# Two scan directions in one ordered list, and a block inverse that sums only the columns a step still changes, in place in one tile

## The chip, the cores and the metric

The kernel runs on one core of one Trainium2 chip. The metric is the device time of one launch in microseconds, lower is better; three runs of the kernel before lie between 3606.57 and 3625.46 us, with a median of 3611.12. Engines are named as the profile does: PE (TensorE), DVE (VectorE), ACT (ScalarE), POOL (GpSimd), SP (SyncE, whose queue issues nearly all DMAs).

## The reference

One layer of a hybrid backbone for 4096 latent and 256 context tokens of width 1024. A modulated, normalised stream is projected once; half of the result feeds a bidirectional RWKV-7 mixer (8 heads of 64, one scan a direction), the other half a gMLP on chunks of 128 tokens; both are gated, concatenated, projected back and added to the input. Cut to what matters here:

```python
def _delta_scan(r, k, v, decay, kk, kka, s0, reverse):
    def step(s, inp):
        r_t, k_t, v_t, w_t, kk_t, b_t = inp
        sa = jnp.einsum('bhvk,bhk->bhv', s, -kk_t)
        s = (s * w_t[:, :, None, :] + sa[..., None] * b_t[:, :, None, :]
             + v_t[..., None] * k_t[:, :, None, :])
        return s, jnp.einsum('bhvk,bhk->bhv', s, r_t)
...
    for d in range(2):
        ...
        y_d, s_d = _delta_scan(r, k_d, v, decay, kk, kk * a, s0[d], reverse=(d == 1))
        y = y + y_d
        bonus = bonus + jnp.sum(r * k_d * p['r_k'][d].astype(f32), axis=-1, keepdims=True) * v
        finals.append(s_d)
...
    y = (y - mu) * lax.rsqrt(var + GN_EPS) * hv(p['gn_w']) + hv(p['gn_b']) + bonus
...
    mixed = jnp.concatenate([y_a * jax.nn.silu(z_a), y_b * jax.nn.silu(z_b)], axis=-1)
    out = mixed @ p['w_out']
    return x + _rmsnorm(out, p['ln_post']) * gate, s_f, s_b
```

The context runs after the latent tokens in this kernel's lists, from a zero state; its final states are outputs.

## The kernel before

**Stages.** Modulation, normalisation, input projection and token shift come first and write their results to DRAM (0 to some 1340 us). Then phase2 runs the forward scan over 34 tiles of 128 tokens and, beside it, the projection for the gMLP (two tiles at a time, `proj`, lines 1031 to 1066). Then phase3 runs the backward scan over the 34 tiles (latent tiles from the last to the first, then the context) with group norm, gating and the output projection (`part`, line 1260). Below, F0 to F33 are the forward tiles and B0 to B33 the backward ones, in the order in which they run.

**One tile.** The recurrence over 64 tokens is solved in closed form, as a triangular system for each head. `prep_ops` makes the gates, the decays, the operands Z and X, and by PE (`ab`, line 769) and a masked product on DVE (`abm`, line 777) the matrices AB, all heads in one 128-partition tile. `invert_ops` then inverts 64x64 unit-triangular blocks. `diag` (line 786) sends the 16x16 diagonal blocks to DRAM by eight DMAs, and `blocks` (line 821) brings them back as rows in Ab. Fifteen steps on DVE (`step0` to `step14`, a product at line 851 and a subtraction at 855 each) invert all the diagonal blocks at once in TP. `keepT` (line 859) and `place` (line 864, eight DMAs) carry the result through DRAM into Qb, `flip` (line 880) transposes it, and four groups of matmuls `mm0` to `mm3` (line 873, each 16 products of 64x64 operands), with `wm` (line 884, masks the first) and `ym0` to `ym2` (line 893, Qb minus the product) between them, sum the series for the blocks off the diagonal. Every one of these works on all 64 columns of a head; ym0 and ym1 write tiles Y, ym2 writes Tt. `scan_ops` applies it to the state S, one 64-token chunk after the other (`zs`, `av`, `xsc`, `tu`, `uv`, `sm`, `ys`, `su`, `so`). `bon` (line 794) is the bonus: q as the weights, two columns of rkb moving; `bonc` (line 798) copies the eight sums a token. In the forward scan ACT copies the output into yt (line 1091) and `keep` (line 1094) stores it to DRAM.

**What sets the order.** `pipeline` collects the parts of all tiles of one direction with a due time, PERIOD (30 units) times the tile's number plus an entry of a table (AT_FWD, AT_PROJ, AT_BWD), sorts them, and emits them under a schedule that keeps this order on each engine and each queue:

```python
            evs += [(self.PERIOD * n + at[k], f) for k, f in parts.items()]
        with self.tc.manual_schedule():
            for _, f in sorted(evs, key=lambda e: e[0]):
                f()
```

So a tile's preparation, inverse and application overlap those of its neighbours within a direction, and a waiting instruction holds all that follows on its engine. DMAs of SP's queue use eight semaphores in turn (DMAHW0 to DMAHW7 in the rows of order below), and one waits for the landing of the one eight before it.

**Between the directions.** phase2 and phase3 have a `scan_setup` and pools of their own. phase3 starts with the broadcast of the gate vector (`load_gp`, lines 1121 to 1125: eight diagonal tiles `dg` on DVE, eight products on PE), loads gn_w and gn_b on ACT's queue (lines 1131, 1136), and loads w_out in eight pieces through one slot `wst`, each split into a rounded part and a rest for two-pass products (`split_w`: DMA line 243, ACT cast line 244, DVE subtraction line 245). Only then comes the second list. `load_state` (lines 583 to 587) fetches and transposes the initial state when the first tile needs it.

## Time and profile before

| | us |
|---|---|
| median of three runs | 3611.12 (3606.57 to 3625.46) |
| the profiled execution | 3635.12 |
| its span | 3633.4 |
| PE busy | 3238.2 (89%) |
| PE weight loads busy | 2692.5 (74%) |
| DVE busy | 2059.3 (57%) |
| ACT busy | 1219.5 (34%) |
| POOL busy | 1005.1 (28%) |

The profile is one execution as the hardware profiler saw it. Engines work beside each other, so busy times don't add up to the span, and matmul ends are modelled. The granted clock of TensorE is 1.00 at full speed. Rows of a timeline give start and duration, and in brackets the idle time of the engine just before and what ended it.

### The profile page before, as it was taken

How to read it: one execution, taken by the hardware profiler on the slowest of the kernel's cores; microseconds unless marked ns; L12 is line 12 of the kernel's file. 1: busy time of each engine (PE TensorE's matmuls, PEld its weight loads, DVE VectorE, ACT ScalarE, POOL GpSimd, SP SyncE). 2: the span in 40 equal slices, each digit the busy share in tenths (PEclk: the TensorE clock that was granted, in tenths of full speed). 3: DMA queues.
4: the chain of work that ended last, by engine and by line, in shares of the span. 5: the costliest groups of instructions: out<-in, count | busy, mean ns of one | idle time of the engine just before them, and what ended most of it. 6: DMA issues, size and time to landing. Idle time of an engine off the chain costs nothing. (4 is left out here: it accounts for less than half of the span.)

```text
span 3633.4 us, 102021 instructions
## 1 busy us (share of the span) xinstructions
PE 3238.2 (89%) x43093; PEld 2692.5 (74%) x43093; DVE 2059.3 (57%) x4969; ACT 1219.5 (34%) x2928; POOL 1005.1 (28%) x1500
## 2 busy tenths in 40 slices
...
GB/s 261 139 194 154 144 184 168 160 99 93 128 87 99 64 117 95 110 103 118 91 119 99 111 109 104 110 55 104 85 108 120 116 116 119 117 112 113 119 116 69
DMA packets 526870, 429.61 MB, mean 118 GB/s; under 512 B 191051, under 2 KB 458187, under 8 KB 519244
## 3 DMA queue, kind: packets, MB, share of 16 engines
...
q14 instruction: 119, 0.97, 0.1%
HBM read 275.46 MB, written 147.46 MB: 116 GB/s over the span
## 5 line engine op out<-in xcount | busy, mean ns | idle before, releaser
L1042 PE MATMUL acc<-hld,wAh 128*128 128x256 f32 x2176 | 434.7, 300 | 13.3 <-DMA hld<-d_h 13.3
L1042 PEld LDWEIGHTS acc<-hld,wAh 128*128 128x128 f32 x2176 | 356.6, 201 | 25.1 <-DMA hld<-d_h 16.2
L1042 PE MATMUL acc<-hld,wAl 128*128 128x256 f32 x1088 | 317.6, 292 | 0.0
L851 DVE TENSOR_TENSOR tm<-TP,Ab 128x48 f32<-128x48 f32 (+13 forms) x1020 | 218.1, 214 | 156.1 <-DMA Ab<-dA 126.6
L777 DVE TENSOR_TENSOR AB<-prep,mask 128x512 f32<-128x512 f32 x272 | 177.1, 683 | 125.1 <-PE prep L769 122.0
L855 DVE TENSOR_TENSOR TP<-TP,tm 128x48 f32<-128x48 f32 (+13 forms) x1020 | 225.4, 221 | 35.1
L1260 PE MATMUL acc<-wAh,mh 128*128 128x512 f32 x544 | 242.1, 445 | 3.0 <-DVE on L1286 2.9
L272 PE MATMUL acc<-hl,wAh 128*128 128x512 f32 (+1 forms) x576 | 226.0, 395 | 0.0
L724 POOL TENSOR_TENSOR q<-q,k 128x512 f32<-128x512 f32 x68 | 97.3, 1431 | 457.5 <-ACT q L719 348.2
L1260 PE MATMUL acc<-wAl,mh 128*128 128x512 f32 x544 | 220.2, 405 | 0.0
L1260 PE MATMUL acc<-wAh,ml 128*128 128x512 f32 x544 | 220.1, 405 | 0.0
L272 PE MATMUL acc<-hh,wAl 128*128 128x512 f32 (+1 forms) x576 | 218.6, 384 | 0.0
L1042 PEld LDWEIGHTS acc<-hld,wAl 128*128 128x128 f32 x1088 | 217.8, 200 | 0.0
L272 PE MATMUL acc<-hh,wAh 128*128 128x512 f32 (+1 forms) x576 | 217.7, 393 | 0.0
L769 PE MATMUL prep<-Z,X 64*64 64x128 f32 x4352 | 169.2, 283 | 47.6 <-DVE X L755 42.0
L272 PE MATMUL acc<-hld,wAh 128*128 128x512 f32 (+1 forms) x576 | 175.9, 389 | 16.5 <-ACT wAh L244 11.7
L758 POOL TENSOR_TENSOR q<-q,r 128x512 f32<-128x512 f32 x68 | 99.0, 1455 | 327.5 <-DVE X L755 241.7
L465 PE MATMUL acc<-wAh,hld 128*128 128x512 f32 x544 | 183.6, 402 | 0.0
L769 PEld LDWEIGHTS prep<-Z,X 64*64 64x64 f32 x4352 | 129.7, 137 | 72.5 <-issue 34.8
L253 ACT COPY win<-acc 128x512 f32<-128x512 f32 (+1 forms) x108 | 60.7, 564 | 351.6 <-PE acc L272 334.7
L873 PE MATMUL inv<-Y,W 64*64 64x64 f32 x4352 | 160.8, 224 | 18.4 <-DVE Y L893 17.9
L465 PE MATMUL acc<-wzh,hld 128*128 128x512 f32 x544 | 176.0, 394 | 0.0
...
## 6 DMA issues: line engine op xcount, KB each, us to landing
...
```

Of the source, the lines that this page charges most:

```text
L253: nc.scalar.copy(w[:, 2 : 2 + n], ps[:, :n])
L272: self.nc.tensor.matmul(ps[:, :n], a[:, k, :], b[:, k, :n], start=(k == 0 and j == 0), stop=(k == NK - 1 and j == 2),)
L465: nc.tensor.matmul(ps, a[:, k, sub], b[:, k % 2, :], start=(k == 0 and j == 0), stop=(k == NK - 1 and j == 2),)
L724: nc.gpsimd.tensor_mul(fl(P["q"]), fl(P["q"]), fl(P["k"]))
L758: nc.gpsimd.tensor_mul(fl(P["q"]), fl(P["q"]), fl(P["r"]))
L769: nc.tensor.matmul(P["pab", pi][hh][o, 128 * p : 128 * p + 128], w, self.slots(P["Z"], p, pi, hh), start=True, stop=True, tile_position=(6 ...
L777: nc.vector.tensor_mul(P["AB"][:, x, 4 * pi : 4 * pi + 4, :], P["pab", pi][hh].rearrange("p (a b) -> p a b", a=4), m)
L851: nc.vector.tensor_mul(tm[:, :nj, :nt], TP[:, js, s : s + 1].to_broadcast([128, nj, nt]), Ab[:, s : s + 1, tt].to_broadcast([128, nj, nt]),)
L855: nc.vector.tensor_sub(TP[:, js, tt], TP[:, js, tt], tm[:, :nj, :nt])
L873: nc.tensor.matmul(ps[h, 64 * j : 64 * j + 64], l(x, h, j), r[h, j, :], start=True, stop=True, tile_position=(64 * x, 64 * x),)
L1042: nc.tensor.matmul(Q["ps", j][:, b, :], x[:, k, :], y[:, k, :], start=(k == 0 and i == 0), stop=(k == NK - 1 and i == 2),)
L1260: nc.tensor.matmul(P["po"][half], a[:, ki, :], b[:, ki % 2, :], start=(ki == 4 and j == 0), stop=(ki == 3 and j == 2),)
```

## The change

**One list.** `scan_setup` runs once. `direction(d)` makes what differs between the directions (moff, the constants ka2 and rkb, a zeroed tile W), for both ahead of the list, on POOL. `forward` and `backward` return their parts, `scans` sorts them together. The first backward tile stands at `turn()`, 1030.14 units, that is 34 periods and 10.14, so that its preparation stands among the steps of the last forward tiles. `origin(1)` and `triangle(1)` set run0, inc and the mask for the second direction in place, on POOL, inside the list. The pieces of w_out are loaded by SP and split by ACT and POOL from 975.6 units on, into two slots in turn, which like gp, gn, zs, x and the rest of the backward buffers are slices of tiles that the projection's inputs leave free. The gn loads move to SP. The states are fetched ahead and the forward state is stored just before B0's first product.

**Columns.** Of four groups of matmuls, mm0 and mm1 now produce 48 of 64 columns, mm2 32 and mm3 16; wm and the ym work on the same columns. wm writes into the direction's W, whose other columns stay zero, and the ym write in place into Tt, whose first 16 columns (the last 16 backward) ACT copies from Qb (`yown`). The tiles Y are gone.

**Bonus.** rkb becomes the weights (32 columns, two of them filled) and q moves with 128 columns, four products into four quarters of the partitions; ACT copies the result out (`bonr`), PE transposes it (`bont`), and `bonc` reads the eight columns.

**Table.** In the forward table `keep`, the store of yt, moves from 70.37 to 42.50.

```diff
+    def turn(self):
+
+        T = self.PERIOD
+        after = (("su1", "zs0"), ("ys1", "zs0"), ("so0", "zs0"), ("so1", "zs1"), ("cum", "gates00"), ("up", "up"))
+        after += tuple((f"abm{i}", "ab0") for i in ("00", "01", "10", "11"))
+        return T * (self.NT // 128) + 3.0 + max(0.0, *(self.AT_FWD[a] + 0.1 - T - self.AT_BWD[b] for a, b in after))
...
+    def direction(self, d):
+
+        nc, io, st = self.nc, self.io, self.sst
+        c = SimpleNamespace(d=d)
...
+        c.W = st.tile([128, 8, 64], F32, name=f"W{d}")
+        nc.gpsimd.memset(c.W, 0.0)
+        c.ka2 = st.tile([128, 4], F32, name=f"kb{d}")
+        c.ka = self.vT[:, 64 + 4 * d : 68 + 4 * d]
+        nc.gpsimd.tensor_scalar(c.ka2, c.ka, -1.0, 2.0, op0=ALU.mult, op1=ALU.add)
+        c.rkb = st.tile([128, 4, 32], F32, name=f"rkb{d}")
+        nc.gpsimd.memset(c.rkb, 0.0)
+        rk = self.vT[:, 72 + 4 * d : 76 + 4 * d]
+        for hh in range(2):
+            sl = slice(64 * hh, 64 * hh + 64)
+            nc.gpsimd.tensor_scalar_mul(c.rkb[sl, :, hh], rk[sl], 0.25)
...
-    def load_state(self, src):
+    def fetch_state(self, t, src):
+        t = self.stio = t[0:64].rearrange("v (p x) -> v p x", p=4)
+        self.nc.sync.dma_start(t.rearrange("v p (h k) -> v p h k", h=2), src.rearrange("(p h) v k -> v p h k", h=2))
+
+    def load_state(self, zero):
         nc = self.nc
-        if src is None:
+        if zero:
             nc.gpsimd.memset(self.S, 0.0)
             return
-        t = self.s1.tile([64, 4, 128], F32, name="stin", tag="q")
-        nc.sync.dma_start(t.rearrange("v p (h k) -> v p h k", h=2), src.rearrange("(p h) v k -> v p h k", h=2))
         ps = self.px.tile([128, 256], F32, name="us", tag="us")
         for p in range(4):
-            nc.tensor.transpose(ps[:, 64 * p : 64 * p + 64], t[:, p, :], self.ident[:64, :64])
...
-        "ys1": 23.38, "sm1": 23.82, "su1": 25.37, "so1": 42.35, "keep": 70.37,
...
+        "keep": 42.50,
...
         def bon():
-            P["pb"] = pb = psum()
-            pbv = pb[:, 0:8].rearrange("t (h p) -> t p h", h=2)
+
+            P["pb"] = psum()
             for p in range(4):
-                nc.tensor.matmul(pbv[:, p, :], P["q"][:, p, :], self.rkb[:, p, :], start=True, stop=True)
+                nc.tensor.matmul(
+                    P["pb"][32 * p : 32 * p + 32, 0:128], c.rkb[:, p, :], P["q"][:, p, :], start=True, stop=True,
+                    tile_position=(0, 32 * p),
+                )
+
+        def bonr():
+            P["br"] = s1.tile([128, 128], F32, name="br", tag="br")
+            nc.scalar.copy(P["br"], P["pb"][:, 0:128])
+
+        def bont():
+            P["pt8"] = psum()
+            nc.tensor.transpose(P["pt8"][:, 0:128], P["br"], self.ident)
 
         def bonc():
             P["bo"] = s2.tile([128, 8], F32, name="bo", tag="bo", bufs=3)
-            nc.vector.tensor_copy(P["bo"], P["pb"][:, 0:8])
+            nc.vector.tensor_copy(
+                P["bo"].rearrange("t (h p) -> t p h", h=2),
+                P["pt8"][:, 0:128].rearrange("t (p x) -> t p x", p=4)[:, :, 0:2],
+            )
 
...
+        cols = lambda a: slice(16 * a, 64) if d == 0 else slice(0, 64 - 16 * a)
+        low = slice(0, 48) if d == 0 else slice(16, 64)
+        own = slice(0, 16) if d == 0 else slice(48, 64)
+        j8 = lambda t: t.rearrange("p (j t) -> p j t", j=8)
+
+        def mm(i, l, r, cc):
             ps = P["pi", i] = self.px.tile([128, 512], F32, name="inv", tag="inv")
             for j in range(8):
                 for x in range(2):
                     h = slice(64 * x, 64 * x + 64)
                     nc.tensor.matmul(
-                        ps[h, 64 * j : 64 * j + 64], l(x, h, j), r[h, j, :],
+                        j8(ps)[h, j, cc], l(x, h, j), r()[h, j, cc],
                         start=True, stop=True, tile_position=(64 * x, 64 * x),
                     )
...
         def wm():
-            P["W"] = s1.tile([128, 8, 64], F32, name="W", tag="W")
             nc.vector.tensor_mul(
-                P["W"], P["pi", 0].rearrange("p (j t) -> p j t", j=8),
-                fl(self.moff).unsqueeze(1).to_broadcast([128, 8, 64]),
+                P["c"].W[:, :, low], j8(P["pi", 0])[:, :, low],
+                fl(P["c"].moff)[:, low].unsqueeze(1).to_broadcast([128, 8, 48]),
             )
-            P["Y"] = self.Qb
+
+        def yown():
+            P["Tt"] = self.s2.tile([128, 8, 64], F32, name="Tt", tag="Tt")
+            nc.scalar.copy(P["Tt"][:, :, own], self.Qb[:, :, own])
 
         def ym(i):
-            tag = "Tt" if i == 2 else "Y"
-            Y = P["Y"] = self.s2.tile([128, 8, 64], F32, name=tag, tag=tag)
-            nc.vector.tensor_sub(fl(Y), fl(self.Qb), P["pi", i + 1])
-            if i == 2:
-                P["Tt"] = Y
+            cc = cols(i + 1)
+            nc.vector.tensor_sub(P["Tt"][:, :, cc], self.Qb[:, :, cc], j8(P["pi", i + 1])[:, :, cc])
 
         order = list(range(15) if d == 0 else range(15, 0, -1))
...
-    def pipeline(self, order, pp, more, at, extra=()):
-
-        evs = list(extra)
+    def pipeline(self, n0, order, c, pp, more, at):
+
+        evs = []
         for n, t0 in enumerate(order):
-            P = dict(t0=t0)
+            P = dict(t0=t0, c=c)
             begin, sink, own = more(n, P)
             parts = {
                 **self.load_ops(P), **self.prep_ops(P, pp), **self.invert_ops(P), **self.scan_ops(P, begin, sink), **own,
             }
-            evs += [(self.PERIOD * n + at[k], f) for k, f in parts.items()]
-        with self.tc.manual_schedule():
-            for _, f in sorted(evs, key=lambda e: e[0]):
...
+    def scans(self):
+
         with ExitStack() as ctx:
             hp = self.pool(ctx, "h2", bufs=3)
             op = self.pool(ctx, "o2", bufs=2)
             pp = self.pool(ctx, "p2", bufs=2, space=PSUM)
-            self.scan_setup(ctx, 0)
-
-            ws = []
+            self.scan_setup(ctx)
+            self.load_up(0)
+            self.origin(0)
+            self.triangle(0)
+            evs = self.forward(hp, op, pp, self.direction(0))
+            evs += self.backward(hp, op, pp, self.direction(1))
+            T, N = self.PERIOD, self.NT // 128
+            evs += [
+                (T * (N - 1) + self.AT_FWD["up"] + 0.01, lambda: self.load_up(1)),
+                (self.turn() + self.AT_BWD["gates00"] - 0.01, lambda: self.origin(1)),
+                (self.turn() + self.AT_BWD["ab0"] - 0.01, lambda: self.triangle(1)),
+            ]
+            with self.tc.manual_schedule():
+                for _, f in sorted(evs, key=lambda e: e[0]):
+                    f()
+
...
+        def load_gp(b):
+            dgs = self.s2.tile([128, 2, 128], F32, name="dg", tag="xs")
+            for half in range(2):
+                pg = pp.tile([128, 512], F32, name="prep", tag="prep")
+                for k4 in range(4):
+                    k = 4 * half + k4
+                    dg = dgs[:, k4 % 2]
+                    nc.vector.tensor_scalar_mul(dg, self.ident, self.gl[:, k, b : b + 1])
+                    nc.tensor.matmul(pg[:, 128 * k4 : 128 * k4 + 128], self.ones, dg, start=True, stop=True)
...
+        def load_w(i):
+            q, half = units[i]
+            src = io["w_out"][0, :, 512 * half : 512 * half + 512]
+            st = box[2 * (i % 2)][:, 0:1024].rearrange("p (k n) -> p k n", k=2)
+            if q < 2:
+
+                v = src[0:512].rearrange("(k a h c) n -> h a c k n", k=2, a=2, h=2)[q]
+                for a in range(2):
+                    nc.sync.dma_start(st[64 * a : 64 * a + 64], v[a])
+            else:
+                nc.sync.dma_start(st, src[256 * q : 256 * q + 256].rearrange("(k p) c -> p k c", p=128))
+
+        def split(i):
+            st = box[2 * (i % 2)][:, 0:1024].rearrange("p (k n) -> p k n", k=2)
+            hi, lo = (self.wA.tile([128, 2, 512], F32R, name=f"wo{x}", tag="wA") for x in "hl")
+            ws[units[i]] = (hi, lo)
+            nc.scalar.copy(hi, st)
+            nc.gpsimd.tensor_sub(lo, st, hi.bitcast(F32))
...
+        at = T * (N - 2) + max(self.AT_PROJ.values()) + 0.1
+        evs += [(at, room), (at + 0.01, lambda: load_gn(0)), (at + 0.02, lambda: load_gn(1)), (at + 10.0, half_gn)]
+        evs += [(at + 0.03 + 6 * i, lambda i=i: load_w(i)) for i in range(8)]
+        evs += [(at + 7.5 + 6 * i, lambda i=i: split(i)) for i in range(8)]
+        evs += [
+            (at + 54.0, lambda: load_gp(0)),
+            (self.turn() + self.AT_BWD["zs0"] - 12.0, lambda: self.fetch_state(box[2][:, 1536:2048], io["state_bwd"][0, 0])),
+            (self.turn() + self.AT_BWD["zs0"] - 0.02, lambda: self.store_state(box[2][:, 1024:1536], io["new_state_fwd"][0, 0])),
+            (self.turn() + T * N + 3 * T, lambda: self.store_state(box[2][:, 1024:1536], io["new_state_bwd"][0, 0])),
...
+                P["bv"] = box[3]
...
+                P["zs"] = box[2][:, 1024:1536]
...
+        order = list(range(self.TS - 128, -1, -128)) + list(range(self.NT - 128, self.TS - 1, -128))
+        evs += self.pipeline(self.turn() / T, order, c, pp, more, self.AT_BWD)
+        return evs
```

On SP, in the forward scan at an odd tile, the store of the output (d_yf) and keepT (dT<-TP) stand like this before:

```order
L657 DMA lw<-d_lora 128x128 [waits PE_49]
L1094 DMA d_yf<-yt 128x512 [waits DMAHW6_49,Activation_49]
L1049 DMA s<-d_s 128x256 [waits DMAHW7_49,DMAHW1_49]
L859 DMA dT<-TP 2x64x128 [waits DMAHW0_49,DVE_49]
L1049 DMA s<-d_s 128x256 [waits DMAHW2_49]
```

and like this after; the store has moved behind a load of the gMLP gate (s) to just ahead of keepT.

```order
L687 DMA lw<-d_lora 128x128 [waits PE_49]
L1121 DMA s<-d_s 128x256 [waits DMAHW7_49,DMAHW2_49,Pool_49]
L1164 DMA d_yf<-yt 128x512 [waits DMAHW0_49,Activation_49]
L904 DMA dT<-TP 2x64x128 [waits DMAHW1_49,DVE_49]
L1121 DMA s<-d_s 128x256 [waits DMAHW3_49]
```

On POOL, at the start of the backward direction, before: the masks come first, then the products q of B0.

```order
L519 AFFINE_SELECT mask<-ones 64x64 [waits DMAHW2_49,PE_49]
L519 AFFINE_SELECT mask<-ones 64x64 [waits Pool_49]
L519 AFFINE_SELECT mask<-ones 64x64 x6
L527 AFFINE_SELECT moff<-ones 64x64 x2
L553 AFFINE_SELECT eye<-ones 64x128 x2
L559 MEMSET Qb 128x512 [waits Pool_49]
L1060 TENSOR_TENSOR s<-s,th 128x256 [waits DMAHW6_49,DMAHW3_49,DVE_49]
L736 COPY gc<-G 128x8
L580 MEMSET S 128x256
L736 COPY gc<-G 128x8 [waits DMAHW3_49,DMAHW4_49,DMAHW2_49,DMAHW5_49,DMAHW1_49,DMAHW6_49,DMAHW0_49,DMAHW7_49,Activation_49,Pool_49]
L724 TENSOR_TENSOR q<-q,k 128x512 [waits DMAHW4_49,Activation_49]
L758 TENSOR_TENSOR q<-q,r 128x512 [waits DMAHW5_49,DVE_49]
```

After, the first subtraction of w_out (wol) stands between B0's two q products, and the selects of the mask behind them:

```order
L755 TENSOR_TENSOR q<-q,k 128x512 [waits DMAHW5_49,Activation_49,Pool_49]
L1236 TENSOR_TENSOR wol<-box_26262,woh 128x1024 [waits DMAHW1_49,DMAHW0_49,Activation_49]
L789 TENSOR_TENSOR q<-q,r 128x512 [waits DMAHW6_49,DVE_49]
L889 COPY TP<-eye 128x128
L558 AFFINE_SELECT mask<-ones 64x64
L558 AFFINE_SELECT mask<-ones 64x64 [waits Pool_49]
L558 AFFINE_SELECT mask<-ones 64x64 x6
```

On SP at the same place, before, the last pieces of w_out and B0's diag (dA<-AB), where each load waits for DVE's subtraction:

```order
L243 DMA wst<-in_w_out 128x2x512 [waits DMAHW5_49,DMAHW4_49,DVE_49]
L243 DMA wst<-in_w_out 128x2x512 [waits DMAHW6_49,DVE_49]
L243 DMA wst<-in_w_out 128x2x512 [waits DMAHW7_49,DMAHW0_49,DVE_49]
L786 DMA dA<-AB 16x8x16 [waits DMAHW1_49,DVE_49]
L786 DMA dA<-AB 16x8x16 x3
L786 DMA dA<-AB 16x8x16 [waits DVE_49]
L786 DMA dA<-AB 16x8x16 x2
```

and after, the second and third piece ahead of B0's diag, where the third waits for POOL; the others have moved ahead of F33's place or behind diag.

```order
L1227 DMA box_26264<-in_w_out 64x2x512 [waits DMAHW4_49]
L1227 DMA box_26264<-in_w_out 64x2x512 [waits DMAHW5_49]
L1227 DMA box_26262<-in_w_out 64x2x512 [waits DMAHW6_49,Pool_49]
L1227 DMA box_26262<-in_w_out 64x2x512 [waits DMAHW7_49]
L1167 DMA d_bf<-bo 128x8 [waits DMAHW0_49]
L817 DMA dA<-AB 16x8x16 [waits DMAHW1_49,DVE_49]
L817 DMA dA<-AB 16x8x16 [waits DMAHW2_49]
```

On PE, in the forward scan, the bonus between the products of the state and the second ab, before:

```order
L970 MATMUL us<-UV,tk 64x64 [waits PE_49]
L970 MATMUL us<-UV,tk 64x64 x7
L794 MATMUL prep<-rkb,q 128x2 [waits DVE_49,Pool_49]
L794 MATMUL prep<-rkb,q 128x2 x3
L769 MATMUL prep<-Z,X 64x128 [waits DVE_49] x2
L769 MATMUL prep<-Z,X 64x128 x14
```

and after, with the transpose behind it; ab's products have moved behind an instruction that waits for ACT.

```order
L1025 MATMUL us<-UV,tk 64x64 [waits PE_49]
L1025 MATMUL us<-UV,tk 64x64 x7
L825 MATMUL prep<-q,rkb_9193 32x128 [waits DVE_49,Pool_49]
L825 MATMUL prep<-q,rkb_9193 32x128 x3
L836 MATMUL prep<-ident,br 128x128 [waits DVE_49,Activation_49]
L800 MATMUL prep<-Z,X 64x128 [waits PE_49]
L800 MATMUL prep<-Z,X 64x128 [waits DVE_49]
L800 MATMUL prep<-Z,X 64x128 x14
```

## Rows read from the trace of the kernel before

**Rows 1.** Head of the page: span and instructions of the profiled execution.
```profile
span 3633.4 us, 102021 instructions
```

**Rows 2.** Windows: from:to length, then busy (instructions) by engine, clock, DMA, GB/s.
```profile
core 0: us, PE busy (x) PEld busy (x) DVE busy (x) ACT busy (x) POOL busy (x), PEclk, DMA share, GB/s
1450.00:2360.00 910.00, 822.29 (x16473) 768.05 (x16471) 581.22 (x1570) 346.73 (x926) 126.78 (x174) 0.97 0.39 107
...
2450.00:2640.00 190.00, 118.46 (x1940) 97.71 (x1942) 107.57 (x276) 67.56 (x165) 44.06 (x68) 0.69 0.36 92
...
2640.00:3530.00 890.00, 815.85 (x14955) 661.96 (x14951) 717.72 (x1948) 430.79 (x1144) 405.19 (x621) 0.98 0.42 116
```

**Rows 3.** Timeline of DVE: first instruction of step0 for F0, F1, F33, B0, B1, B2.
```profile
1379.48 0.18 DVE L851 TENSOR_TENSOR tm<-TP,Ab 128x15 f32<-128x15 f32 x1 [3.86 <-DMA Ab<-dA]
...
1414.51 0.15 DVE L851 TENSOR_TENSOR tm<-TP,Ab 128x15 f32<-128x15 f32 x1
...
2416.12 0.17 DVE L851 TENSOR_TENSOR tm<-TP,Ab 128x15 f32<-128x15 f32 x1 [2.54 <-DMA Ab<-dA]
...
2511.16 0.17 DVE L851 TENSOR_TENSOR tm<-TP,Ab 128x15 f32<-128x15 f32 x1 [7.89 <-DMA Ab<-dA]
...
2547.58 0.17 DVE L851 TENSOR_TENSOR tm<-TP,Ab 128x15 f32<-128x15 f32 x1
...
2579.71 0.17 DVE L851 TENSOR_TENSOR tm<-TP,Ab 128x15 f32<-128x15 f32 x1
```

**Rows 4.** Chain of waits between the scans: start, duration, what held the end.
```profile
2468.51 1.05 ACT wAh L244
...
2471.49 4.08 DMA wst<-in_w_out
...
2497.29 3.66 DMA wst<-in_w_out
...
2503.91 7.16 DMA Ab<-dA
```

**Rows 5.** Instructions by line on POOL: busy us, mean ns, then idle before.
```profile
L218 POOL TENSOR_TENSOR hl<-ht,hh 128x512 fp32r<-128x512 f32 (+1 forms) x72 | 94.0, 1320 | 96.4 <-ACT hh L217 96.4
L519 POOL TENSOR_SCALAR_AFFINE_SELECT mask<-ones 64x64 f32<-64x64 f32 x16 | 3.8, 235 | 4.3 <-PE acc L465 3.6
```

**Rows 6.** Timeline of DVE: the forward state's copy, and a diagonal of load_gp.
```profile
1412.10 0.42 DVE L587 COPY S<-us 128x256 f32<-128x256 f32 x1 [7.46 <-PE us L586]
...
2464.93 0.29 DVE L1121 TENSOR_SCALAR dg<-ident,gl 128x128 f32<-128x128 f32 x1 [1.16 <-PE prep L1122]
```

**Rows 7.** Timeline of SP and DVE: the DMA part of backward tile B16's loop.
```profile
3012.15 0.54 SPq L821 DMA_DIRECT2D Ab<-dA  x1
...
3016.47 0.68 DVE L893 TENSOR_TENSOR Tt<-Qb,inv 128x512 f32<-128x512 f32 x1
...
3018.00 0.17 DVE L851 TENSOR_TENSOR tm<-TP,Ab 128x15 f32<-128x15 f32 x1 [0.85 <-DMA Ab<-dA]
```

**Rows 8.** Timeline of PE in the forward scan: bursts of the inverse, of ab, of bon.
```profile
2219.50 1.15 PE L873 MATMUL inv<-Qb,W 64*64 64x64 f32 x32
...
2243.28 1.10 PE L769 MATMUL prep<-Z,X 64*64 64x128 f32 x32
...
2245.28 1.02 PE L794 MATMUL prep<-rkb,q 128*128 128x2 f32 x8 [0.27 <-DVE AB L777]
```

**Rows 9.** Timeline of ACT and SP: an even forward tile (two rows), then an odd one.
```profile
2200.19 0.74 ACT L1091 COPY yt<-xy 64x256 f32<-64x256 f32 x2
...
2206.76 0.54 SPq L859 DMA_DIRECT2D dT<-TP  x1
...
2238.17 0.54 SPq L859 DMA_DIRECT2D dT<-TP  x1
...
2240.33 0.75 ACT L1091 COPY yt<-xy 64x256 f32<-64x256 f32 x2
...
2242.07 3.75 SPq L864 DMA_DIRECT2D Qb<-dT  x8
...
2248.43 5.50 SPq L786 DMA_DIRECT2D dA<-AB  x8
```

576 lines of the change are left out of this document (280 added, 296 removed), and 49 rows, old and new, of tables (AT_BWD, AT_FWD).

## The prediction

> **What bounds the kernel now.** I read the page first: a span of 3633.4 us [rows 1]. The windows by stage come next [rows 2]. They tempt one to call the kernel TensorE-bound: PE is busy 822 of 910 us in the forward scan and 816 of 890 in the backward scan, DVE only 581 and 718. The third window, between the scans, is different: PE is busy 118 of 190 us and its clock falls to 0.69. I call it the seam.
>
> The DVE timeline shows the beat of both scans [rows 3]. The first instruction of the block inverse (step0, line 851) of forward tile F1 starts at 1414.51 and that of the last, F33, at 2416.12: 32 periods of 31.3 us. The backward tiles go as fast: B2 at 2579.71, B16 at 3018.00 [rows 3, 7], 14 periods of 31.3. From F33 to B0, however, there are 95.0 us, and from B0 to B1 36.4.
>
> What sets the 31.3 is a loop that rows 7 and 9 let one follow: step0 and the 14 steps after it on DVE, further DVE work up to the last masked product (abm, line 777) of the next tile, eight DMAs to DRAM (diag, line 786), one DMA back (blocks, line 821), and step0 of the next tile, which waits for that landing. In rows 7 blocks is issued at 3012.15 and step0 starts at 3018.00, after DVE has idled 0.85 us for Ab; the last subtraction of the inverse (ym2, line 893) ended before that. So PE's 90% is cover, not bound, and what DVE does between diag and step0 is cover as well, as long as step0 still waits for Ab.
>
> The seam is a chain of its own [rows 4]. The output weights go through one staging slot: load, cast on ACT (1.05), subtraction on DVE, then the next load. From the load at 2471.49 to the one at 2497.29 there are four such turns of 6.45 us, some 4 of them a landing. B0's blocks stand on SP behind the loads, at 2503.91, and land 7.2 us later.
>
> **The seam.** After the change there is one ordered list, so that B0's preparation runs under F33's steps and the loads begin at once behind F33's store of its diagonal blocks. An undisturbed turn would be one period, 31.3 us. On top of it I put what now stands in B0's way. On POOL, between B0's q product and its mask, there is the first subtraction, 128x1024, twice the 1.32 us of 128x512 at line 218, and then eight selects of 0.235 that turn the mask round [rows 5]: 2.64 + 1.88 = 4.5, and abm of B0 on DVE waits for the last of them. On SP four gn loads and eight halves of w_out stand between F33's keepT and B0's blocks: 12 issues at 0.54, as line 821 took one [rows 7], are 6.5, of which about 1 lies where place waits for keepT's landing anyway. 31.3 + 4.5 + 5.5 = 41.3; I take 41, so 95.0 - 41 = **-54**. Bounds: if POOL's piece is hidden, 31.3 + 5.5 = 36.8, say 36 (-59). If one load that waits for its slot to be free (landing 4.08, cast 1.05, subtraction 2.64, together 7.8) is waited out in front of diag, where the third load indeed waits for POOL, 49, say 50 (-45).
>
> From B0 to B1 the other four loads move into B0's and B1's turns. I put that distance at 32.5, near B1 to B2's 32.1 [rows 3]: **-3.9** (-4 to +6, the price of one waited load, which rival C uses). The broadcast of the gate vector (load_gp) leaves the gap and enters DVE's part of B1's loop: eight diagonals of 0.29 [rows 6]. Without waits that is 2.3 us; with the 1.16 that DVE idled before one for PE [rows 6], 8 x 1.45 = 11.6. I take **+3.5**, nearer the low end, since there are two slots now and a product can run under the next diagonal.
>
> **The start.** The state load of the forward scan was issued in the middle of F0, and DVE sat 7.46 us behind its transposes [rows 6]; F0 to F1 took 35.0 instead of 31.3 [rows 3]. It is now fetched 30 units before the tile, so I give back 3.5: **-3.5** (0 to -5). The constants of both directions are now built by POOL ahead of the list, some six more small ones at about 0.24 [rows 5]: **+1** (0 to 3).
>
> **The column cut.** On DVE the four instructions behind the matmuls (lines 884 and 893) go from 512 columns to 384, 384, 256 and 128. A 128x512 takes 0.68 [rows 7] and a PSUM read of 128x256 0.42 [rows 6], about 1.0 ns a column, so 0.13 + 0.13 + 0.26 + 0.40 = 0.9 us a tile. In the backward scan all of it stands between diag and step0, where step0 waits for Ab anyway: worth the few tiles in which it does not. I take **-2** for the direction (-6 to +6: a new wait could come with the copy of the own columns, which now stands on ACT ahead of the products). On PE 256 columns a pair of operands become 144, but that costs the same: 32 matmuls of line 873 on 64 columns take 1.15 us and 32 of line 769 on 128 columns 1.10, and eight of line 794 on 2 columns 1.02 [rows 8]. I count zero.
>
> **The forward scan.** Here one wait goes and one comes. ym2 stands among the next tile's steps, so its 0.4 us is on the loop: -0.4 in every tile. But the store of yf (line 1094) is moved from after the next tile's turn to right before keepT (line 859) on SP, and it waits for ACT's copy into yt (line 1091). SP is in order: behind it wait keepT, the loads of UV, the eight place DMAs (line 864) and diag. In even tiles the copy ended at 2200.93 and keepT came at 2206.76 [rows 9]: nothing. In odd tiles, where the copy stands behind the gMLP gate, keepT was issued at 2238.17 and the copy ended at 2241.08 [rows 9]: 2.9 us of waiting, with the store's own issue 3.4. Place ended at 2245.82, one further issue behind it ends at 2246.4, and diag began at 2248.43 [rows 9], so 2.0 of it is slack: +1.4, less ym2's 0.4; this tile's copy is a late one, and I take +0.8. 17 x (-0.4) + 17 x 0.8 = **+7** (-14, if slack swallows it all, to +16, if half a microsecond of it is missing).
>
> **The bonus.** Four weight loads of q with 2 columns become four of the small weights with 128, an ACT copy and a transpose. PE gets through the eight old instructions in 1.02 [rows 8]; the new detour lies behind the masked products, and in the forward scan diag waits for place longer than for AB, in the backward scan bonc stands behind diag. I count zero.
>
> The Trainium skill speaks against that: "TensorEngine Tiling (Array Packing)", section Key Properties, says that a change of the tiling mode, not only of the tile, drains the engine. The trace shows at most 0.27 us of idle PE before line 794, and that is put down to DVE [rows 8]; it neither proves nor excludes a drain. By the rule the sum would get rival D's addition.
>
> **Sum.** -54 - 3.9 + 3.5 - 3.5 + 1 - 2 + 7 = -51.9. The profiled execution took 3635.1 us with what lies around its span, 24.0 above the median of 3611.1; the sum is made against the former, 3583.2, and carried to the median: **3559 us**.
>
> **Rivals.**
>
> A (slower than before): the yf store blocks SP in every tile, not only in odd ones. It would then cost the 3.5 us in full 34 times, 119, against the -58.9 of the other terms: 3611 + 60 = 3671. It decides from 58.9/34 = 1.7 us a tile. For it: SP is in order and everything of the loop's DMA part is queued behind. Against it: 5.8 us of room in even tiles and 2.1 of slack in odd ones [rows 9].
>
> B (the column cut pays): if PE's time went by columns, a tile would save 0.44 x 4.6 = 2.0 us, half of it perhaps on the path: 68 us, 3491. Against it: 128 columns took no longer than 64 [rows 8], and step0 waits for a DMA [rows 7].
>
> C (the seam half closes): SP stands on two waited loads, 2 x 7.8, in front of B0's diag and blocks: 57 instead of 41, and B0 to B1 42. The sum is -38 + 5.6 - 3.5 + 1 - 2 + 7 = -30, **3581**. For it: the loads now share a queue with the loop's DMAs, and two slots are still only two. Against it: the splits run on ACT and POOL, and POOL has little to do at this place.
>
> D (array shapes): the bonus changes the shape of the array from 64x64 weights to 128x32, to 128x128 and back. Were each tile to pay 0.27 us [rows 8] on the path, 68 x 0.27 = 18: 3577. Against it: bon isn't what diag waits for.
>
> **How the numbers follow.** Forecast 0.63, C 0.19, D 0.08, A 0.05, B 0.05. The range: the lower bounds of the terms add up to -34 (seam -5, forward -21, backward -4, start and gate -4), which gives 3525. The upper ones, without the wait from B0 to B1, which is C's, add up to +39 (seam +9, forward +9, backward +8, start and gate +13): 3598. C and D lie inside; A and B outside, and some tails: I give 3525 to 3598. What a measurement here can tell from no change is about 0.5%, 18 us, so faster means below 3593. Forecast and B are faster nearly throughout, C and D mostly: 0.86 faster, 0.08 within, 0.06 slower (A and a little).
>
> **What would show it.** In the profile after, step0 of F33 to step0 of B0 should read about 41 us, B0 to B1 32 to 33, F0 to F1 about 31.5, and the clock in the seam should stay near that of the scans. In forward tiles SP should stand about 3 us at the yf store in odd tiles only, with a two-tile period about 0.4 us longer than 62.6. In the backward scan the period should stay 31.2 to 31.3, with DVE idling longer before step0, and the four bursts of line 873 should take as long as now. I am wrong if step0 of B0 waits for the w_out splits, if the store holds even tiles too, or if the backward period moves by over 0.2 us: then the loop isn't where I put it.

## The result, and the profile after

The changed kernel takes 3585.41 us (median of six runs, 3580.05 to 3592.26) against 3609.98 for the kernel before in the same comparison: a ratio of 0.9933 (0.9911 to 0.9954), or 24.6 us less. That is faster by under 1%, with an interval that ends below 1; it lies inside the range, and 51.9 us less had been forecast. The page of the profiled execution (3583.4 us):

```profile
span 3581.7 us, 102504 instructions
PE 3205.5 (89%) x43161; PEld 2636.8 (74%) x43161; DVE 2000.9 (56%) x4945; ACT 1245.8 (35%) x3064; POOL 1046.4 (29%) x1521
```

The span is 51.7 us below that of [rows 1], just what the sum said (51.9), and it misleads: the first profile of the kernel before was a long one (the first experiment). The windows of the same three stages, columns as in [rows 2]:

```profile
core 0: us, PE busy (x) PEld busy (x) DVE busy (x) ACT busy (x) POOL busy (x), PEclk, DMA share, GB/s
1450.00:2360.00 910.00, 811.56 (x16545) 748.10 (x16537) 558.24 (x1568) 357.07 (x986) 128.80 (x175) 0.96 0.38 107
...
2400.00:2540.00 140.00, 90.38 (x1654) 77.14 (x1649) 72.58 (x194) 49.51 (x122) 43.07 (x49) 0.60 0.37 96
...
2590.00:3480.00 890.00, 806.92 (x15065) 642.98 (x15062) 701.35 (x1953) 447.80 (x1213) 425.00 (x624) 0.98 0.42 117
```

The seam is shorter, but its granted clock did not rise, against the prediction's sign that it would stay near that of the scans: it is 0.60 over 140 us, most of it at the lower of the two levels, after a scan at 0.96 in which PE was busy 812 of 910 us. From step0 of F33 to that of B2, the same stretch of work in every profile, it is 0.57; the two profiles of the kernel before have 0.59 and 0.61. The timeline of DVE, first instruction of step0 of F0, F1, F33, B0, B1, B2 and B32, which answers to [rows 3]:

```profile
1378.22 0.17 DVE L896 TENSOR_TENSOR tm<-TP,Ab 128x15 f32<-128x15 f32 x1 [3.34 <-DMA Ab<-dA]
...
1408.49 0.17 DVE L896 TENSOR_TENSOR tm<-TP,Ab 128x15 f32<-128x15 f32 x1 [1.30 <-DMA Ab<-dA]
...
2408.26 0.17 DVE L896 TENSOR_TENSOR tm<-TP,Ab 128x15 f32<-128x15 f32 x1 [4.24 <-DMA Ab<-dA]
...
2456.47 0.17 DVE L896 TENSOR_TENSOR tm<-TP,Ab 128x15 f32<-128x15 f32 x1 [8.53 <-DMA Ab<-dA]
...
2498.75 0.17 DVE L896 TENSOR_TENSOR tm<-TP,Ab 128x15 f32<-128x15 f32 x1
...
2537.43 0.17 DVE L896 TENSOR_TENSOR tm<-TP,Ab 128x15 f32<-128x15 f32 x1 [0.95 <-DMA Ab<-dA]
...
3467.12 0.17 DVE L896 TENSOR_TENSOR tm<-TP,Ab 128x15 f32<-128x15 f32 x1 [0.57 <-DMA Ab<-dA]
```

F33 to B0 is 48.2 us instead of 95.0, but B0 to B1 grew from 36.4 to 42.3 and B1 to B2 from 32.1 to 38.7. The same distances, read in the same way from every profile, carry the rest of this text (us; "again" is the kernel before a second time, e14 is the same file as e8, the other columns are explained where they come up):

| | before | again | after | e3 | e4 | e8 | e14 | e15 | e17 | e18 | e10 |
|---|---|---|---|---|---|---|---|---|---|---|---|
| F0 to F1 | 35.0 | 35.9 | 30.3 | 29.8 | 30.5 | 30.6 | 30.7 | 30.8 | 30.0 | 31.3 | 30.5 |
| F1 to F33 | 1001.6 | 984.0 | 999.8 | 1011.9 | 962.6 | 959.3 | 952.0 | 968.5 | 962.3 | 953.5 | 952.2 |
| F33 to B0 | 95.0 | 94.9 | 48.2 | 49.3 | 46.5 | 44.9 | 47.9 | 48.0 | 45.2 | 48.7 | 39.8 |
| B0 to B1 | 36.4 | 36.5 | 42.3 | 41.6 | 42.5 | 40.6 | 42.8 | 42.0 | 42.3 | 42.8 | 39.2 |
| B1 to B2 | 32.1 | 31.1 | 38.7 | 39.5 | 38.4 | 38.1 | 41.0 | 38.8 | 38.4 | 39.2 | 41.1 |
| B2 to B32 | 938.3 | 926.0 | 929.7 | 931.9 | 931.8 | 921.3 | 920.3 | 915.4 | 923.9 | 933.3 | 926.3 |

### The profile page after: what moved, and what is told of

Same layout as the page of the kernel before. It is cut to its first block, busy times and chain, and to the rows that moved or that the text cites. A ratio compares the mean times of both kernels' runs of the same rounds, so it can differ in the third digit from the quotient of the medians.

```text
span 3581.7 us, 102504 instructions
## 1 busy us (share of the span) xinstructions
PE 3205.5 (89%) x43161; PEld 2636.8 (74%) x43161; DVE 2000.9 (56%) x4945; ACT 1245.8 (35%) x3064; POOL 1046.4 (29%) x1521
## 4 chain that ended last, share of the span: by engine, by line
PE 52%; DMA 20%; DVE 15%; SPq 7%; issue 3%; ACT 2%; POOL 1%; POOLq 0%; DVEq 0%; ACTq 0%
PE acc L273 19%; PE acc L466 10%; DMA Ab<-dA 9%; PE acc L1357 5%; DVE TP L900 5%; DVE tm L896 5%; PE acc L1113 4%; DMA dA<-AB 4%; SPq L817 4%; PE prep L800 3%; SPq L909 2%; DMA box<-in_x_sample 2%; DVE AB L808 1%; PE us L1012 1%; DVE cum L742 1%
## 5 line engine op out<-in xcount | busy, mean ns | idle before, releaser
L1357 PE MATMUL acc<-woh,box 128*128 128x512 f32 x1088 | 405.0, 424 | 4.1 <-DVE box L1383 4.1
L1357 PEld LDWEIGHTS acc<-woh,box 128*128 128x128 f32 x1088 | 210.2, 193 | 65.7 <-issue 10.7
L1357 PE MATMUL acc<-wol,box 128*128 128x512 f32 x544 | 219.7, 404 | 0.0
L273 PE MATMUL acc<-hld,wAh 128*128 128x512 f32 (+1 forms) x576 | 175.5, 388 | 14.7 <-DMA wst<-in_w_in 9.9
L800 PE MATMUL prep<-Z,X 64*64 64x128 f32 x4352 | 168.8, 283 | 15.6 <-DVE X L786 13.9
L1020 ACT ACTIVATE UV<-us 64x256 f32<-64x256 f32 x272 | 102.9, 378 | 212.5 <-PE us L1012 208.2
L1012 PE MATMUL us<-xs,Tt 64*64 64x64 f32 x2176 | 105.7, 232 | 77.6 <-DVE tm L896 65.0
```

The costliest lines, as they stand in the source:

```text
L273: self.nc.tensor.matmul(ps[:, :n], a[:, k, :], b[:, k, :n], start=(k == 0 and j == 0), stop=(k == NK - 1 and j == 2),)
L800: nc.tensor.matmul(P["pab", pi][hh][o, 128 * p : 128 * p + 128], w, self.slots(P["Z"], p, pi, hh), start=True, stop=True, tile_position=(6 ...
L1012: nc.tensor.matmul(P["pu", pi][h, half(p)], P["Tt"][h, 4 * pi + p, :], P["xs", pi][h, half(p)], start=True, stop=True, tile_position=(h.st ...
L1020: nc.scalar.mul(P["UV"][h, pi, hh, :], P["pu", pi][h], -1.0)
L1357: nc.tensor.matmul(P["po"][half], a[:, ki, :], b[:, ki % 2, :], start=(ki == 4 and j == 0), stop=(ki == 3 and j == 2),)
```

## Experiments

**e1_before_again: the kernel before, unchanged.**

> The kernel before, unchanged, to get a second profile of it. The profiled executions of before and after are 51.7 us apart (3635.1 and 3583.4), as forecast, the medians only 24.6 (3610.0 and 3585.4). Theory 1: the first profiled execution of before was an unusually slow one, by some 25 us that lie in one stage; then this profile reads a span near 3608 and shows which distance between first steps is shorter than in the first profile (F33 to B0 was 95.0 us, F0 to F33 1036.6, B2 to B33 970.0, the part before F0 1379.5). Theory 2: profiling itself costs this kernel 25 us, whichever execution is looked at; then the span reads 3625 to 3640 again, with all distances as in the first profile, and the timed runs stay near 3610.

Measured: 3605.48 us, ratio 1.0003 (0.9980 to 1.0027), profiled span 3602.8, which is 30.6 below that of [rows 1]. The timeline of DVE in this profile, step0 of F1, F33 and B2:

```profile
1414.14 0.15 DVE L851 TENSOR_TENSOR tm<-TP,Ab 128x15 f32<-128x15 f32 x1
...
2398.13 0.17 DVE L851 TENSOR_TENSOR tm<-TP,Ab 128x15 f32<-128x15 f32 x1 [2.81 <-DMA Ab<-dA]
...
2560.53 0.18 DVE L851 TENSOR_TENSOR tm<-TP,Ab 128x15 f32<-128x15 f32 x1 [1.80 <-DMA Ab<-dA]
```

F1 to F33 is 984.0 here against 1001.6, B2 to B32 926.0 against 938.3; F33 to B2, all of the seam, is 162.4 against 163.6. Two profiles of one program differ by up to 18 us in a scan, and a stage is judged against both columns from here on. The seam isn't always that steady: e8 and e14, one file, have 123.6 and 131.7 from F33 to B2. Against this second profile the changed kernel is 15.8 us *slower* in the forward scan and 3.7 in the backward one.

**e4_store_late and e3_full_columns: the forward scan.** e4 puts the store of yf back behind the next tile's turn, except in the last three tiles, where the seam needs it early:

```diff
-            evs += [(self.PERIOD * (n0 + n) + at[k], f) for k, f in parts.items()]
+            late = lambda k: 70.37 - 42.50 if c.d == 0 and k == "keep" and n < 31 else 0.0
+            evs += [(self.PERIOD * (n0 + n) + at[k] + late(k), f) for k, f in parts.items()]
```

> The changed kernel with the forward store of yf back at 70.37 in the table for all tiles but the last three. Theory 1: the store ahead of keepT costs the odd tiles; keepT then comes 0.24 us behind the last step instead of 2.0 to 4.0, diag about 1 us earlier in odd tiles, and the forward scan (F1 to F33, 999.8 us) shortens by 10 to 20 us; even tiles unchanged. Theory 2: the wait is hidden, because diag of an odd tile then waits for AB (ready 10.5 us behind the last step) or for its landing; within 4 us.

Measured: 3557.22 us, ratio 0.9863 (0.9827 to 0.9898): 28 us less, and 37 in F1 to F33. The timeline of DVE, ACT and SP in an odd forward tile of the changed kernel, from the last step on (DVE's last step, ACT's copy, then the store, keepT, place and diag on SP):

```profile
2227.49 0.18 DVE L900 TENSOR_TENSOR TP<-TP,tm 128x8 f32<-128x8 f32 x1
...
2229.84 0.74 ACT L1161 COPY yt<-xy 64x256 f32<-64x256 f32 x2
...
2230.61 0.32 SPq L1164 DMA_DIRECT2D d_yf<-yt  x1
2231.02 0.54 SPq L904 DMA_DIRECT2D dT<-TP  x1
...
2234.28 4.72 SPq L909 DMA_DIRECT2D Qb<-dT  x8
...
2239.57 2.22 SPq L817 DMA_DIRECT2D dA<-AB  x3
```

and of the same tile in e4:

```profile
2192.69 0.17 DVE L900 TENSOR_TENSOR TP<-TP,tm 128x8 f32<-128x8 f32 x1
...
2192.89 0.53 SPq L904 DMA_DIRECT2D dT<-TP  x1
...
2196.19 3.64 SPq L909 DMA_DIRECT2D Qb<-dT  x8
2199.93 0.37 SPq L1122 DMA_DIRECT2D s<-d_s  x1
2203.24 1.72 SPq L817 DMA_DIRECT2D dA<-AB  x4
```

With the store early, keepT is issued 3.35 us after the last step instead of 0.03, because SP stands at the store until ACT's copy is there. From step to diag it is 11.9 against 10.4 us: of the 3.3 lost and the 1.1 that place is longer, 2.9 (2200.30 to 2203.24 in e4) were slack, and 1.5 reach diag. On the mean of the 16 odd tiles between F1 and F33 keepT is issued 2.53 us after the end of the last step (0.03 in e4 and in the kernel before), diag 11.20 against 9.67, and the odd period is 32.39 against 30.14; even periods are 30.10 and 30.02. That is 2.25 us in 16 odd tiles, 36 us, nearly all of the difference. So 1.5 of it reach diag, and 0.7 more come between diag and the next step0. SP's queue waits between 1600 and 2300 us (who waits, for whom: us in total, times, longest) show the store at ACT's last product of a chunk, 12 times, and at its copy, 7 times (most of this time lies before the last step has ended and costs nothing):

```profile
SPq L1164 <- ACT UV L1020: 114.9, 12, 10.8
...
SPq L1164 <- ACT yt L1161: 10.9, 7, 2.8
```

e3 undoes the column cut, and with it ACT's copy of the own columns, with the store early and the new bonus:

```diff
-        cols = lambda a: slice(16 * a, 64) if d == 0 else slice(0, 64 - 16 * a)
-        low = slice(0, 48) if d == 0 else slice(16, 64)
+        cols = lambda a: slice(0, 64)
+        low = slice(0, 64)
...
-            nc.scalar.copy(P["Tt"][:, :, own], self.Qb[:, :, own])
```

> The changed kernel with all 64 columns again in the four products, in wm and in the subtractions (still in place in Tt, without the copy of the own columns). Theory 1, as forecast: on PE the columns cost nothing (bursts stay at 1.06 to 1.15 us), on DVE the last subtraction comes back with 0.4 us into the forward loop, and nothing in the backward one: forward +0.4 a tile, +14 us, backward 0 to +2. Theory 2: the cut is worth nothing anywhere, within 4 us. Theory 3: it carries the backward scan too, where DVE is the fuller engine (718 of 890 us): backward +0.3 or more a tile, +25 us in all.

Measured: 3595.69 us, ratio 0.9972 (0.9953 to 0.9991): the cut is worth 10 us here. The profiles have 12 between F1 and F33 and 2 in the backward scan, less than two profiles of one program can differ. What doesn't vary is a forward tile from the start of step0 to the end of step14: 8.60 us with the cut and 9.01 without, in e8 and e15 too (8.60 and 9.02); that is the 0.4 of ym2, as forecast.

**e2, e5, e6, e7: the seam.** e2 gives POOL's subtractions of w_out to DVE:

```diff
-            nc.gpsimd.tensor_sub(lo, st, hi.bitcast(F32))
+            nc.vector.tensor_sub(lo, st, hi.bitcast(F32))
```

> The changed kernel, with the subtraction of the w_out pieces on DVE instead of POOL at the same places of the list. Theory 1: in the seam DVE is held by POOL's 2.35 us subtractions (a state product of 0.43 took 2.55, a Z product of 0.68 took 2.87 while one ran), so without them F33 to B0 falls from 48.2 to about 45, B0 to B1 from 42.3 to about 39, B1 to B2 stays near 38.7; 5 to 8 us less in all, although DVE gets eight instructions of 1.24. Theory 2: the seam waits for SP's queue (place behind ten loads) and not for DVE; then DVE's added 9.9 us show, and the time stays or rises by up to 8 us.

Measured: 3578.79 us, ratio 0.9926 (0.9903 to 0.9949), not to be told from after's 0.9933. F33 to B0 is 47.7 against 48.2, F33 to B2 126.7 against 129.2.

The next three stand on e4. e5 moves the gate's broadcast to a later place, e6 loads gn later and the first four pieces of w_out into four staging slots behind F33's place, so that no load stands between its keepT and its place, e7 does both and gives the subtractions to DVE where it waits:

```diff
-            (at + 54.0, lambda: load_gp(0)),
+            (self.turn() + 19.5, lambda: load_gp(0)),
```

> The version with the late store (median 3557.2; F33 to B0 46.5, B0 to B1 42.4, B1 to B2 38.5), with the broadcast of the gate vector moved from among B1's steps to where DVE waits for B2's blocks. Theory 1: load_gp is what makes B1 to B2 7 us longer than a period; that distance falls to 31 to 33 and the next stays a period: -6 us. Theory 2: the transient of the turn itself lengthens it (clock 0.66, PE late); then B1 to B2 falls by at most 2.

```diff
-        evs += [(at + 0.03 + 6 * i, lambda i=i: load_w(i)) for i in range(8)]
+        evs += [(x, lambda i=i: load_w(i)) for i, x in enumerate((980.6, 980.9, 981.2, 981.5, 1002.0, 1002.3, 1002.6, 1024.5))]
```

> The version with the late store, with the gn loads moved behind the seam and the first four w_out pieces loaded into four slots behind F33's place, in front of B0's diag, so that no load stands between keepT and place or between diag and blocks; splits on POOL as before. Theory 1 (SP's queue holds the seam): F33 to B0 falls from 46.5 by 4 to 7 us, as place of F33 no longer waits for load slots (flip came 13.7 us behind the last step instead of 10.5) and blocks no longer for a piece. Theory 2 (DVE held by POOL, PE at half clock): falls by under 2.

> The late store, the gate vector moved, the loads behind place in four slots, and the splits' subtractions on DVE in the stretches in which DVE waits for B0's and B1's blocks. If the seam's surplus over three periods (127 - 94 = 33 us) is made of the queue, POOL's hold on DVE and the gate vector, then F33 to B0 reads 37 to 41, B0 to B1 33 to 36, B1 to B2 31 to 33, and the median 3535 to 3542. If instead the halved clock of PE in the seam makes the surplus, the three distances stay above 115 us and the median above 3547.

Measured: e5 3547.96 (0.9837, 0.9803 to 0.9870), with B1 to B2 down from 38.4 to 33.9; e6 3558.89 (0.9861, 0.9836 to 0.9887), F33 to B2 124.9 where e4 has 127.4; e7 3556.68 (0.9853, 0.9825 to 0.9881), 123.9, with F33 to B0 at 42.0 but B1 to B2 at 41.5, although the gate is moved there too. None of the four is told from its base by its time, and F33 to B2 moves by less than the 8 us between e8 and e14. What the traces do show is that each wait that is named goes where it is taken away (B1's fifteen steps, between which the gate's work stands, take 16.6 us in e4 and 8.8 in e5; DVE's idle time before F33's flip falls from 4.87 us in the changed kernel to 1.08 in e6), and that little of it reaches the end.

In the changed kernel they are these. SP (loads of w_out, F33's place, B0's blocks) and DVE (F33's flip) between the scans:

```profile
2421.79 1.31 SPq L1227 DMA_DIRECT2D box<-in_w_out  x2
...
2424.49 5.47 SPq L909 DMA_DIRECT2D Qb<-dT  x8
...
2431.51 0.71 DVE L931 STREAM_TRANSPOSE Tb<-Qb 128x512 f32<-128x512 f32 x1 [4.87 <-DMA Qb<-dT]
```

then a state update on DVE beside a subtraction of w_out on POOL:

```profile
2439.38 2.36 POOL L1236 TENSOR_TENSOR wol<-box,woh 128x1024 fp32r<-128x1024 f32 x1
...
2439.46 2.55 DVE L1040 TENSOR_TENSOR S<-S,gc 128x256 f32<-128x256 f32 x1
```

and, in the chain of waits, the two halves of the gate's products (the granted clock is 0.60 in that stretch):

```profile
2501.88 2.37 PE prep L1206 x8
...
2504.29 2.08 PE prep L1206 x8
```

So F33's own place stands behind the loads: it begins 6.0 us after keepT, 3.6 in even tiles of the scan, and DVE is idle 4.87 us for it. The DVE product, 0.43 us elsewhere, takes 2.55 and ends 0.27 after POOL's instruction; a 0.68 product at 2468.26 takes 2.87 beside the next subtraction. The Trainium skill, "SBUF — State Buffer", section SBUF: two separate sides, states this: DVE with two SBUF inputs and a POOL instruction that reads SBUF take a shared port pair as an exclusive lock for a whole instruction. The trace agrees with it.

A fourth wait none of the runs takes away. F33 is an odd tile, and the store of yf stands ahead of its keepT (DVE's last step, ACT's copy, the store, keepT):

```profile
2415.18 0.17 DVE L900 TENSOR_TENSOR TP<-TP,tm 128x8 f32<-128x8 f32 x1
...
2417.27 0.74 ACT L1161 COPY yt<-xy 64x256 f32<-64x256 f32 x2
...
2418.03 0.33 SPq L1164 DMA_DIRECT2D d_yf<-yt  x1
2418.47 0.54 SPq L904 DMA_DIRECT2D dT<-TP  x1
```

keepT is issued 3.1 us after the last step, 0.08 in the kernel before. e4 leaves the store early in the last three tiles, so every version from the changed kernel to e18 has these 3.1 us between F33 and B0.

**e8, e14, e16, e9, e12, e13: the bonus.** e8 is e4 with the bonus of the kernel before, e14 the same file again, e16 the changed kernel (store early) with that bonus:

```diff
-                nc.tensor.matmul(
-                    P["pb"][32 * p : 32 * p + 32, 0:128], c.rkb[:, p, :], P["q"][:, p, :], start=True, stop=True,
-                    tile_position=(0, 32 * p),
-                )
+                nc.tensor.matmul(pbv[:, p, :], P["q"][:, p, :], c.rkb[:, p, :], start=True, stop=True)
...
-            nc.scalar.copy(P["br"], P["pb"][:, 0:128])
...
-            nc.tensor.transpose(P["pt8"][:, 0:128], P["br"], self.ident)
```

> The version with the late store, with the bonus as before (q as weights, two moving columns, no transpose). Forecast: no difference within 4 us, since bon isn't what diag waits for. Rival D (array shapes cost): 0.27 us a tile, 18 us faster than the late store alone. A third: the old form's PE time of 1.02 us instead of 0.43 + 0.33 comes back into the loop, up to 10 us slower.

> The version with late store and old bonus once more, as the base of the next two and to see how far two runs of one kernel lie apart: median 3520 to 3535, backward period 30.7 to 30.9, forward mean 29.8 to 30.0.

> The changed kernel with the old bonus and nothing else (the store stays early). If the costs of the store and of the new bonus add up, the median falls from 3585.4 by the 20 to 30 us that the bonus cost behind the late store, to 3555 to 3565; if the store's wait covers the bonus in the forward scan, only the backward part shows, 10 us: 3575.

Measured: e8 3527.52 (0.9775, 0.9742 to 0.9809), e14 3529.36 (0.9770, 0.9739 to 0.9801), 28 to 30 us below e4; e16 3572.91 (0.9905, 0.9876 to 0.9934), 12.5 below after, though its interval overlaps after's. The forecast counted the bonus at nothing. Read the other way, the early store costs 28 us with the new bonus (e4 to after) and 44 with the old one (e8 and e14 to e16). The timeline of ACT and DVE in a backward tile of e4 shows bonr waiting for PE, and two instructions of DVE that then wait for POOL:

```profile
2922.91 0.27 ACT L832 COPY br<-prep 128x128 f32<-128x128 f32 x1 [0.70 <-PE prep L825]
...
2926.31 0.75 DVE L1384 SCALAR_TENSOR_TENSOR box<-acc,rso,box 128x512 f32<-128x512 f32 x1 [0.89 <-POOL box L1393]
...
2927.94 0.69 DVE L1317 TENSOR_TENSOR yt<-yt,box 128x512 f32<-128x512 f32 x1 [0.55 <-POOL yt L1314]
```

Behind bonr on ACT stand casts and norms whose results POOL turns into these operands. DVE's waits from 2560 to 3400 us in e4 and then in e8 (us in total, times, longest):

```profile
DVE box L1384 <- POOL box L1393: 24.0, 27, 0.9
...
DVE tm L896 <- DMA Ab<-dA: 16.3, 12, 2.4
```

```profile
DVE tm L882 <- DMA Ab<-dA: 29.6, 25, 4.1
...
DVE box L1370 <- POOL box L1379: 1.6, 1, 1.6
```

In e8 step0 still waits for Ab in 25 of 27 tiles, in e4 in 12: in the others DVE itself is late there. Which part of the bonus does it, three runs asked. e9 moves the copy behind the norms in the backward table (`bonr` from -39.89 to -34.90, `bont` and `bonc` behind it); e12 keeps the old products and adds only a copy on ACT that waits for PE; e13 adds only the four products of 32 columns and a transpose on PE.

> The version with the late store and the new bonus (median 3557.2; backward period 31.08), with the bonus's ACT copy behind the group norm's on ACT in the backward scan, its transpose and DVE copy moved with it. Theory 1: the new bonus costs the backward scan because its copy waits 0.7 us for PE on ACT with the cast of mb and the norms queued behind it; POOL's rest, sum and weighting come late, and DVE waits 0.9 us for one and 0.55 for the other, so that step0 no longer waits for Ab in half of the tiles. Then the backward period falls to 30.7 to 30.8 as with the old bonus (30.73), the two DVE waits on POOL vanish, and the span falls by about 10 us. Theory 2: the PE work of the new form (shapes, transpose) costs it; then the period stays at 31.0 to 31.1.

> Late store and old bonus, and one ACT copy of its eight columns behind it, at the place where the new bonus has its copy: the copy waits for PE, nobody reads its result. Theory 1 (a wait in ACT's queue costs): the backward period rises from 30.75 to about 31.05, the forward mean by 0.2 to 0.4, 15 to 25 us in all, as with the new bonus. Theory 2 (PE's part costs): within 0.1 a tile of the base.

```diff
+            P["br"] = s1.tile([128, 8], F32, name="br", tag="br")
+            nc.scalar.copy(P["br"], P["pb"][:, 0:8])
```

> Late store and old bonus, and beside it PE's instructions of the new form: four products of 32 columns of weights with q moving and a transpose of a constant, at the places of the new bonus, into columns that nobody reads. Theory 1 (a wait in ACT's queue costs): within 0.1 a tile of the base. Theory 2 (array shapes, rival D): the period rises by 0.3 a tile or more, 18 us.

Measured: e9 3552.46 (0.9851, 0.9828 to 0.9874), not to be told from e4; B2 to B32 is 935.1 against 931.8. The copy's own wait for PE (19.0 us in 27 tiles) and DVE's second wait for POOL (14.7) are gone and step0 waits for Ab in 21 tiles, but DVE's 25.6 us at POOL (box) stayed and the scan is no shorter, so the copy's place in ACT's order alone isn't the cause. e12 3572.96 (0.9874, 0.9831 to 0.9917) and e13 3570.85 (0.9879, 0.9848 to 0.9910): each part alone costs more, 41 to 44 us over e14, than the whole bonus does. Parts that cost more than their sum mean that something else moved with them: in the compiled programs the tiles TP, AB and Ab of the next paragraph begin at a multiple of 256 bytes in e14, 32 bytes past one in e12, and 192 in e13, as in e4.

**e17_new_bonus_shifted and e18_old_bonus_shifted: the place of the tiles.** In the compiled programs the tiles TP and AB, from which keepT and diag read, and Ab begin at a multiple of 256 bytes in e8, e14 and e16, and 192 bytes past one in after and e4 (the new bonus has larger constants and the tile br, 1472 bytes a partition in all). These two runs add nothing but an unused tile of 64 bytes a partition behind the constants of the bonus, to e4 and to e8:

```diff
+        if d:
+            st.tile([128, 16], F32, name="pad")
```

> Late store and new bonus (median 3557.2; backward period 31.08, forward mean 30.08), with an unused tile of 64 bytes behind the bonus's constants: every scan tile after it moves by 64 bytes in a partition, and the blocks' tiles (Ab, TP, AB) stand at multiples of 128 bytes, as with the old bonus, instead of 64 off. Theory 1 (the new bonus's work costs): nothing changes, 3550 to 3562. Theory 2 (its larger constants moved the tiles, and DMAs land later at the new places): landings fall from 4.9 to 4.75 us in the backward scan, the periods to 30.7 and 29.8, the median to 3530 to 3540.

> Late store and old bonus (3527.5 and 3529.4; backward period 30.7, forward mean 29.8), with the same unused tile of 64 bytes, so that the blocks' tiles stand 64 bytes off a multiple of 128, as in the changed kernel. Theory 1 (the new bonus's work costs): nothing changes, 3522 to 3535. Theory 2 (the tiles' places cost): landings rise by 0.15 to 0.2 us, the median to 3545 to 3560.

| median us (ratio) | TP, AB, Ab at a multiple of 256 | 64 bytes off one of 128 |
|---|---|---|
| old bonus | e8 3527.5 (0.9775), e14 3529.4 (0.9770) | e18 3548.4 (0.9842, 0.9809 to 0.9875) |
| new bonus | e17 3541.4 (0.9823, 0.9791 to 0.9856) | e4 3557.2 (0.9863, 0.9827 to 0.9898) |

Across, 64 bytes cost 20 us with the old bonus and 16 with the new one; down, the new bonus costs 13 and 9. Of the four only the 20 is clear of the noise (the intervals of e14 and e18 don't overlap); in the other three pairs the intervals overlap. The timeline of DVE, step0 of B2 and B32, in e8 and in e18:

```profile
2494.45 0.17 DVE L882 TENSOR_TENSOR tm<-TP,Ab 128x15 f32<-128x15 f32 x1
...
3415.79 0.17 DVE L882 TENSOR_TENSOR tm<-TP,Ab 128x15 f32<-128x15 f32 x1 [0.60 <-DMA Ab<-dA]
```

```profile
2497.66 0.18 DVE L884 TENSOR_TENSOR tm<-TP,Ab 128x15 f32<-128x15 f32 x1 [1.09 <-DMA Ab<-dA]
...
3430.93 0.17 DVE L884 TENSOR_TENSOR tm<-TP,Ab 128x15 f32<-128x15 f32 x1 [0.74 <-DMA Ab<-dA]
```

921.3 and 933.3 us; e14 has 920.3, and e17 923.9 against e4's 931.8. The forward scan doesn't show it (962.3 and 962.6; 953.5 beside 959.3 and 952.0). What is slower is the way through DRAM: from keepT to the first place DMA a backward tile takes 3.15 us in e8, e14 and e17, and 3.30 in e4 and 3.32 in e18; from the end of the issue of blocks to Ab's landing, where step0 waits for it, 4.75, 4.74 and 4.72 against 4.88 and 4.94. The other profiles of changed kernels fall in with this: with the tiles at a multiple of 256 (e10, e11, e15, e16) the way to place takes 3.15 or 3.16 and B2 to B32 915 to 927 us, at 192 past one (after, e2, e3, e5 to e7, e9, e13) 3.30 or 3.31 and 930 to 940, and in e12 3.39 and 943. DVE's waits differ with the bonus, not with the place: 24.0 us at POOL in e4 and 23.7 in e17. Other tiles move along, so which tile matters isn't settled. The Trainium skill, "DMA: Bandwidth & Descriptors", section How a descriptor splits into AXI transactions, says that a read of a DMA has to begin at a 256-byte boundary, so that a descriptor that doesn't also fetches the bytes ahead of it. For keepT's reads the direction agrees, with 0.15 to 0.17 us; for the landing of Ab, which is written, it says nothing.

**e15, e10, e11: what is left.** e15 is e8 with all 64 columns; e10 is e8 with the gate moved as in e5, loads behind place as in e7, and seven of the eight subtractions on DVE; e11 is e10 with idle products of 128 columns on PE in the seam (the expectation says 180; the trace has 192).

> Late store and old bonus (3527.5 and 3529.4 in two runs; forward 959.3 and 952.0, backward 921.3 and 920.3), with all 64 columns again. What the column cut is worth where no store wait and no new bonus cover it. Theory 1 (as forecast: the last subtraction in the forward loop, nothing else): forward +0.4 a tile, 13 us, backward 0 to 2. Theory 2: it is worth twice as much, 25 us or more, because DVE's chain behind diag is part of the loop in both scans, and the copy of the own columns costs nothing.

> Late store, old bonus, gate vector moved to where DVE waits for B2's blocks, loads of w_out behind place in four slots, seven subtractions on DVE where it waits for B0's and B1's blocks, the eighth on POOL. The separate runs read 46.5 to 42.0 for F33 to B0 (the order of loads and subtractions), 42.4 to 40 for B0 to B1 and 38.5 to 33.9 for B1 to B2 (the gate vector). If these add up, the three distances read about 116 instead of 124 (old bonus alone: 44.8, 40.7, 38.1), and the median is 8 us below the old bonus's 3527.5, about 3520. If the moved pieces only push each other, it stays at 3525 to 3530.

> The combined version with idle work for PE in the seam: 180 products of constants into an unused buffer, at the places in the order where the output projection of three more backward tiles would stand (their result is read by nobody). Theory 1: the rest of the seam's surplus over three periods (some 22 of 116 us) is PE at half its clock, which the trace shows at 0.50 to 0.70 for 140 us there; with the filler the granted clock stays above 0.9, F33 to B0 falls below 39, B0 to B1 below 36, B1 to B2 to 32, and the total falls by 10 to 20 us. Theory 2: the surplus is waits (loads, copies, DVE); then the clock rises and the distances do not fall, or grow by the filler's own time.

Measured: e15 3529.66 (0.9783, 0.9754 to 0.9813), no different from e8, though the profile gives it 9 to 17 us more in the forward scan and 5 to 6 less in the backward one. With the store late and the old bonus the cut is worth nothing that can be measured. e10 3518.77 (0.9751, 0.9726 to 0.9777) is the lowest time of all, but its interval overlaps those of e8 and e14: F33 to B2 is 120.1 us against 123.6 and 131.7. e11 3521.76 (0.9761, 0.9735 to 0.9788). Windows of e10 and e11 over the seam, columns as above:

```profile
2360.00:2490.00 130.00, 91.20 (x1524) 80.44 (x1521) 75.67 (x206) 49.68 (x120) 25.03 (x36) 0.61 0.41 107
```

```profile
2360.00:2490.00 130.00, 115.42 (x2003) 105.93 (x1998) 73.54 (x200) 47.72 (x114) 26.47 (x42) 0.89 0.38 100
```

With more products in it the granted clock rises from 0.61 to 0.89, and F33 to B2 is 121.8 us, not less. So either the clock doesn't hold the seam or the filler takes as much as it gives back; a gain below the 8 us between e8 and e14 can't be excluded.

## Why the prediction was right in sign and wrong in size

Against the second profile of the kernel before, whose time is near the median, the span falls by 21.1 us:

| term | forecast | measured against "again" (against the first) |
|---|---|---|
| up to F1 (state load, constants) | -3.5, +1 | -5.7 (-6.0) |
| F1 to F33 | +7 | +15.8 (-1.8) |
| F33 to B0 | -54 | -46.7 (-46.8) |
| B0 to B1 | -3.9 | +5.8 (+5.9) |
| B1 to B2 (gate) | +3.5 | +7.6 (+6.5) |
| B2 to B32 | -2 | +3.7 (-8.6) |

The rest lies behind B32.

**The base.** The prediction knew that its profile was 24 us above the median and carried the difference over. The terms taken from distances stayed exposed: it took the scans for 31.3 us a tile, where the second profile has 30.75 forward and 30.87 backward. So the profiles before and after agreed with the sum by chance.

**The seam** holds most of the gain, as forecast: the store, the state and the list do what they say, and 95 becomes 48. But its three distances were to fall by 54.4 us (-54, -3.9, +3.5) and fell by 33 to 34: 20 of the 27 us that are missing lie here. The step that failed is the price of what stands in B0's and B1's way. F33 to B0 was taken for 41, with 50 as the upper bound of one waited load, and the trace has 48.2. There the loads hold up F33's own place, which the prediction never set behind them, the store of yf holds F33's keepT 3.1 us, which the prediction had as 1.2 in the mean odd tile of the scan, and POOL's subtractions hold DVE, where it saw only POOL's own time (2.36 each, 2.64 forecast). So its own sign of being wrong, step0 of B0 waiting for the w_out splits, holds in part: the product that takes 2.55 us stands in the chain ahead of B0's diag. B0 to B1 was to be 32.5 and came out at 42, the figure of rival C; at F33 to B0 C said 57, too much. C's sum leaves out the gate's +3.5; with it C would have read 3585, the measured time, but out of other distances. The gate's work makes B1's fifteen steps 6.8 us longer (15.6 against 8.8 before and in e5), within its 2.3 to 11.6.

How much each of these waits is worth in the end isn't shown: with most of them taken away (e10) F33 to B2 is 120.1 us, against 129.2 in the changed kernel and 123.6 and 131.7 in e8 and e14, on which e10 stands, where three scan periods are 92 to 94. What else holds these three tiles is open.

**The forward store** was seen in the right tiles and for the right reason (odd ones, by ACT's copy), and rival A's case, the store in every tile, is out: even periods are unchanged by it. The term was mis-sized. The prediction took 1.2 a tile for the store, 20 us; e4 shows 2.25, or 36 us, in the profile and 28 by the medians. Up to diag the working was nearly right: in the mean odd tile keepT comes 2.5 us later, the slack in front of diag falls from 2.1 to 0.8, and 1.5 reach diag, where +1.4 had been worked out. The 0.7 behind diag had no term; e16 against e8, with the old bonus, has the 1.5 and not the 0.7, and its cause is open. What made up for some of it is that the rest of the change gains more here than ym2's 0.4 a tile: without the early store and the new bonus (e8, e14) F1 to F33 is 25 to 32 us below the second profile. Some 15 of this remain without the column cut (e15); what gives them isn't shown.

**The column cut** is worth 10 us as it stands (e3) and nothing that can be measured in the better version (e15). Rival B, 68 us, is out. The four DVE instructions are shorter as forecast, and that they stand beside the way through DRAM is the likely reason; no run shows it by itself.

**The bonus** is the step that was wrong in kind: a term put at nothing. It was weighed on PE alone, by diag; what stands behind bonr on ACT and where its constants push the other tiles were not asked. Behind the late store it costs 28 to 30 us: 9 to 13 by its work and 16 to 20 because the tiles lie off a multiple of 256 bytes, which no view of a profile names. Only the place with the old bonus, 20, is clear of the noise by itself. How the work costs isn't shown: DVE's 24 us at POOL stand in e17 too, whose backward scan is within 4 us of e8's, and e9 gained nothing. With the store early work and place together are worth 12.5 by the medians (e16), not 28 to 30: costs of one loop don't add up. Rival D, 18 us by array shapes, has about the right size and an unproven cause: e13, which was to show it, has its tiles 192 bytes past a multiple of 256 as e4 has, and its interval overlaps those of e4 and e18.
